# Seven products for the pooling gate, in a new product order, with stores on the POOL queue

## The chip, the cores and the metric

The kernel runs on one core of one Trainium2 chip. The metric is the device time of one execution in microseconds (us), lower is better. The core's engines have queues of their own and meet through semaphores: PE (TensorE, matmuls; PEld is its weight load), DVE (VectorE), ACT (ScalarE), POOL (GpSimd) and SP (SyncE, which here only issues transfers). ACT and POOL can issue transfers too.

## The reference

One decoder block on 1024 tokens of width 1024, in float32. Cut to what matters here:

```python
h = rms_norm(x, norm_gain) * (1.0 + scale) + shift
proj = h @ w_in
q, k, v, z_a, u, z_b, m_a, m_b = split(proj)          # 1024 columns each
p_a = (stick_breaking_attention(q, k, v) * silu(z_a)) @ w_branch_a
pooled = multiscale_causal_pool(u)    # window means over 2, 4, 8, 16 positions minus u, a linear map, a scale
p_b = (pooled * silu(z_b)) @ w_branch_b
merged = sigmoid(m_a) * p_a + sigmoid(m_b) * p_b
out = rms_norm(x + gate * (merged @ w_out), final_gain)   # gate comes from c, through w_gate
```

## The kernel before

Every large product is made of three float32r matmuls: both operands are split into a high part (a cast, on ACT) and a low part (the difference, on DVE), and high·high, high·low and low·high are added up in a PSUM bank. One matmul is 128 x 128 by 128 x 512.

After the norm the kernel goes through five stages, one behind the other on PE. They carry the names of their PSUM tiles in the profile:

- `u`: projection of the pooling input, copied out to DRAM (`u_d`) by ACT.
- `vp`: projection v, `mp`: projection m_b, each by `seven`: a 1024 x 1024 x 1024 product as Strassen and Winograd do it, with seven products of 512-blocks for eight. Its products are called p1 to p7.
- `wzb`: the pooling gate z_b, by `project`: all eight blocks, 16 x 24 = 384 matmuls. Beside it `make_d` forms the window differences d on DVE (log2 of the window adds on `win` tiles, L546, and a subtraction, L550), silu and the product with d follow per tile (L738, L739), and the sums of gate blocks that the next stage needs (`t1`, `t2`, L743 to L746). A product of w_gate's rows with silu(c) (`wg`, `sg`, L749 to L752) is spread over it.
- `bp`: pooled·silu(z_b) times w_branch_b, again `seven`; results go to DRAM as `pb_d`.

Behind them come the projections of q, k and the rest (`p`), the attention, and the output products.

In `seven(nm, sums, load, b_of, ...)` each product has two halves q = 0, 1 over the contraction, 24 matmuls each; the whole has 7 x 48 = 336. The operand a of a half is a quarter load (128 x 1024) or a sum of such loads, the operand b a quarter of h, of differences of h (`ht`), or of the gate. `raw(first, ...)` gives the tile for a load: with first = 1 from the tag `raw` in the pool `wts` (two buffers), otherwise from the tag `ar` in the stage's own pool (two buffers). The pool `vs` of v and m lies where the pool `first` lay, which holds the weights of u (`wg`). `a_op` makes the high and low part in a tile `whl` of two buffers (L559 the cast on ACT, L560 the difference on DVE), `b_op` the same for b (L565, L566). `copied` takes a PSUM bank to SBUF (ACT, L609), `added` adds one (DVE, L573), and `final` is the stage's own way out: `values` (vo, to `v_d`), `gate_b` (sigmoid, to `sb_d`), `branch` (to `pb_d`).

The order of the products is the loop's: p1, p5, p6, p7, p4, p3, p2. The order on each engine's queue is that of a scheduler which fills the queues from the program text by its own costs; only where the code says `keep_in_program_order` is it fixed. All loads and the stores v_d, sb_d, pb_d are issued on SP.

## Time and profile before

| | us |
|---|---|
| median of 3 runs (lowest, highest) | 1188.6 (1188.01, 1190.27) |
| the profiled execution | 1187.59 |
| its span in the profile | 1185.8 |
| PE busy | 1169.2 |
| DVE busy | 832.4 |
| ACT busy | 588.3 |
| POOL busy | 216.7 |
| mean granted TensorE clock | 0.998 of full speed |

The profile is that of one execution. Rows of a timeline give start, duration, engine, line, operation, out<-in with buffer numbers left out, and in brackets the idle time ahead of it with what ended it. Rows of groups give the busy time and the mean duration in ns of one instruction. Line L101 is that of a helper through which all matmuls and a few other operations go, so there the tile names tell them apart.

### The profile page before, as it was taken

To read this page: it belongs to the slowest core of one execution; us is meant where nothing else is said; L and a number is where in the kernel's file an instruction comes from. 1 tells how busy PE (TensorE), PEld (TensorE's weight loads), DVE (VectorE), ACT (ScalarE), POOL (GpSimd) and SP (SyncE) were. 2 spreads that over 40 slices of the span, in tenths; PEclk is the share of its full clock that TensorE was granted. 3 is DMA by queue.
4 is the path that set the end of the run, shared out by engine and by line. 5 is a ranking of instruction groups with operands and counts; after the bars stand their busy time and mean duration, and the time that the engine had idled before them with its cause. 6 is when DMAs were issued, how large, how long until landed. Compare 5 with 4: busy or idle time off the path is not lost.

```text
span 1185.8 us, 15373 instructions
## 1 busy us (share of the span) xinstructions
PE 1169.2 (99%) x5602; PEld 975.0 (82%) x5602; DVE 832.4 (70%) x1072; ACT 588.3 (50%) x1137; POOL 216.7 (18%) x248
## 2 busy tenths in 40 slices
PE   8999999999999999999999999999999999999997
...
GB/s 349 257 193 62 180 103 318 187 162 234 200 103 176 97 179 222 79 81 91 84 98 90 62 121 54 135 62 103 94 88 99 37 72 208 349 280 157 213 70 73
DMA packets 74750, 172.49 MB, mean 145 GB/s; under 512 B 9393, under 2 KB 22833, under 8 KB 72498
## 3 DMA queue, kind: packets, MB, share of 16 engines
q1 hardware_dynamic: 68770, 160.82, 41.6%
q10 hardware_dynamic: 5904, 10.68, 2.5%
...
## 4 chain that ended last, share of the span: by engine, by line
PE 84%; DVE 7%; DMA 3%; issue 3%; ACT 2%; SPq 0%; POOL 0%; POOLq 0%; DVEq 0%; ACTq 0%
PE p L101 24%; PE wzb L101 7%; PE mp L101 6%; PE vp L101 6%; PE bp L101 6%; PE o L101 6%; PE pa L101 5%; PE u L101 5%; PE z L101 5%; PE av L101 4%; PE wt L101 4%; PE ua L101 3%; DVE om L942 2%; DVE be L101 2%; PE wm L101 1%
## 5 line engine op out<-in xcount | busy, mean ns | idle before, releaser
L101 PE MATMUL p<-hT,w 128*128 128x512 f32 x1536 | 392.7, 392 | 1.3 <-DVE klo L101 1.3
L101 PEld LDWEIGHTS p<-hT,w 128*128 128x128 f32 x1536 | 283.0, 188 | 59.5 <-DVE klo L101 1.7
L942 DVE TENSOR_TENSOR_SCAN om<-om,eye 128x511 f32<-128x511 f32 (+7 forms) x128 | 184.0, 1442 | 68.9 <-ACT om L938 68.3
L149 POOL TENSOR_TENSOR w<-w_raw,w 128x256 fp32r<-128x256 f32 x124 | 124.8, 1037 | 571.5 <-ACT w L146 571.5
L938 ACT ACTIVATE om<-z 128x512 f32<-128x512 f32 (+2 forms) x192 | 95.0, 495 | 109.2 <-PE z L101 46.8
L962 DVE TENSOR_TENSOR wt<-wt,wt 128x512 fp32r<-128x512 f32 (+1 forms) x160 | 99.0, 619 | 15.7 <-ACT wt L961 14.7
L101 PE MATMUL av<-wt,vv 128*128 128x512 f32 x320 | 106.0, 412 | 0.1
L961 ACT CAST wt<-wt 128x512 fp32r<-128x512 f32 (+1 forms) x160 | 88.2, 551 | 35.0 <-PE wt L101 34.8
L101 DVE TENSOR_TENSOR be<-be,om 128x512 f32<-128x512 f32 (+7 forms) x128 | 98.5, 775 | 0.0
L101 PE MATMUL wt<-ident,be 128*128 128x128 f32 x576 | 90.3, 274 | 3.9 <-DVE wt L962 3.1
L939 ACT ACTIVATE be<-z 128x512 f32<-128x512 f32 (+2 forms) x192 | 94.0, 489 | 0.0
L101 PE MATMUL pa<-ga,wa 128*128 128x512 f32 x384 | 89.9, 390 | 0.9 <-DVE s L1115 0.8
L101 PE MATMUL o<-wo,mhl 128*128 128x512 f32 (+1 forms) x408 | 89.6, 377 | 0.0
L101 PE MATMUL wzb<-hT,wzb 128*128 128x512 f32 x384 | 87.2, 389 | 0.0
L101 PEld LDWEIGHTS pa<-ga,wa 128*128 128x128 f32 x384 | 71.9, 188 | 16.5 <-issue 1.2
L101 PEld LDWEIGHTS o<-wo,mhl 128*128 128x128 f32 x408 | 73.5, 188 | 14.1
L101 PEld LDWEIGHTS wt<-ident,be 128*128 128x128 f32 x576 | 69.5, 140 | 18.7 <-DVE wt L962 6.2
L101 PEld LDWEIGHTS wzb<-hT,wzb 128*128 128x128 f32 x384 | 72.1, 188 | 15.0
L991 POOL TENSOR_TENSOR tp<-tp,tl 128x256 f32<-128x256 f32 x32 | 38.1, 1190 | 153.9 <-DVE tp L988 153.9
L101 PE MATMUL z<-kl,q 128*128 128x512 f32 (+2 forms) x192 | 65.5, 341 | 0.0
L101 PE MATMUL z<-kh,q 128*128 128x512 f32 (+2 forms) x192 | 64.1, 334 | 0.0
L101 PE MATMUL u<-hT,wg 128*128 128x512 f32 x240 | 55.5, 391 | 0.0
...
## 6 DMA issues: line engine op xcount, KB each, us to landing
w_raw<-in_w_in SPq DMA_DIRECT2D x32, 512.0 KB, 3.5
v_d<-vo SPq DMA_DIRECT2D x16, 512.0 KB, 4.2
...
wa_raw<-in_w_branch_a SPq DMA_DIRECT2D x16, 512.0 KB, 4.7
...
va<-in_w_v SPq DMA_DIRECT2D x10, 512.0 KB, 4.0
ma<-in_w_mb SPq DMA_DIRECT2D x10, 512.0 KB, 4.4
```

What stands on the lines that cost most here:

```text
L101: ins = op(*args, **kw)
L149: gp.tensor_tensor(hl[:, 1, es], raw[:, es], hl[:, 0, es].bitcast(F32), op=ALU.subtract)
L938: act.activation(om[:, 1 + b0:1 + b0 + n], zp[:, :n], AF.Sigmoid, scale=-0.125)
L939: act.activation(be[:, b0:b0 + n], zp[:, :n], AF.Sigmoid, scale=0.125)
L942: v.tensor_tensor_scan(om[:, 1:W], om[:, 1:W], eye[:, :W - 1], 0.0, ALU.mult, ALU.max)
L961: act.copy(wt[:, 0, :off], pt[:, :off])
L962: v.tensor_sub(wt[:, 1, :off], pt[:, :off], wt[:, 0, :off].bitcast(F32))
L991: gp.tensor_add(tp, tp, tl)
```

## The change

- The gate z_b becomes a stage of `seven`, called z, with the tiles `zp…`; its results lie in four quarters (`g00` and three of the `ht` tiles), and b takes its operands from them (`g_parts`).
- The order of the products is p1, p2, p6, p7, p5, p4, p3. p1's a11 is loaded into an `ar` tile and kept: p6's operand is s2k = a22 − (a11 − a21), formed in `a_s2`, p7's is a11 − a21, p5's is s2k + a11, loaded once more as a11s. A stage has 14 quarter loads, before 18.
- Within a half the matmuls of the high parts of the first three (q = 0) or two (q = 1) output tiles come first.
- Stores of v, pb and g, and the loads of u, w_gate and d, are issued on POOL (`gp.dma_start`), stores of sb on ACT. A tick, a one-column POOL operation on a result of a given product (`beside`), comes ahead of each load of u and w_gate.
- The window differences are formed in stage v (3, 0, 2, 1) and stage m (5, 7, 6, 4), written to a new DRAM tile `d_d` and read back for z.

The diff, cut to its core:

```diff
@@ load_u, make_d
-        nc.sync.dma_start(u[:, :S], u_d[j])
+        tc.keep_in_program_order(gp.dma_start(u[:, :S], u_d[j]))
...
-        dhls[j] = d
+        gp.dma_start(d_d[j], d)
@@ seven
+        a11 = {}
+
+        def a_11(q):
+            a11[q] = raw(0, 0, 0, q, "a11")
+            return a11[q]
+
+        def a_s2(q):
+            r = raw(1, 1, 0, q, "a21")
+            v.tensor_sub(a11[q], a11[q], r)
+            r = raw(1, 1, 1, q, "a22s")
+            v.tensor_sub(k2(s2k, q), r, a11[q])
+            return k2(s2k, q)
+
         def a_s1(q):
-            r, w = raw(1, 1, 0, q, "a21"), raw(0, 1, 1, q, "a22")
-            v.tensor_add(r, r, w)
-            w = raw(0, 0, 0, q, "a11s")
-            v.tensor_sub(k2(s2k, q), r, w)
-            return r
-
-        def a_s3(q):
-            r, w = raw(1, 0, 0, q, "a11d"), raw(0, 1, 0, q, "a21d")
-            v.tensor_sub(r, r, w)
+            r = raw(1, 0, 0, q, "a11s")
+            v.tensor_add(r, r, k2(s2k, q))
             return r
...
-            p1=lambda q: raw(1, 0, 0, q, "a11"), p5=a_s1, p6=lambda q: k2(s2k, q), p7=a_s3,
-            p4=lambda q: raw(1, 1, 1, q, "a22"), p3=a_s4, p2=lambda q: raw(1, 0, 1, q, "a12"),
+            p1=a_11, p2=lambda q: raw(1, 0, 1, q, "a12"), p6=a_s2, p7=a11.get,
+            p5=a_s1, p4=lambda q: raw(1, 1, 1, q, "a22"), p3=a_s4,
...
-        for name in ("p1", "p5", "p6", "p7", "p4", "p3", "p2"):
-            c = {"p5": "b", "p3": "b", "p2": "c"}.get(name, "a")
+        for name in ("p1", "p2", "p6", "p7", "p5", "p4", "p3"):
+            c = {"p2": "c", "p5": "b", "p3": "b"}.get(name, "a")
...
+                ahead = 3 - q
+                parts_ = [(j, e, 0, 0) for j in range(ahead) for e in range(2)]
                 for j in range(4):
+                    for e in range(2):
+                        parts_ += [(j, e, w, m) for w, m in ((0, 0), (0, 1), (1, 0))[j < ahead:]]
...
+            for do in beside.get(name, ()):
+                gp.tensor_scalar(tick, mark[:, :1], 1.0, 0.0, op0=ALU.mult, op1=ALU.add)
+                do()
@@ stages
+        seven("v", vs, loads("w_v"), h_parts("v"), True, *banks, values, True, pooled(p1=(3,), p6=(0,), p7=(2,), p4=(1,)))
+        seven("m", vs, loads("w_mb"), h_parts("m"), False, *banks, gate_b, True, pooled(p1=(5,), p6=(7,), p7=(6,), p4=(4,)))
...
+        sg = gp_.tile([P, D], F32, name="sg")
+        nc.sync.dma_start(sg, a["c_row"].broadcast_to([P, D]))
+        act.activation(sg, sg, AF.Silu)
+
+        def modulated(j):
+            wg_ = gp_.tile([P, D], F32, tag="wg", bufs=2, name=f"wgt{j}")
+            tc.keep_in_program_order(gp.dma_start(wg_, a["w_gate"][j]))
+            v.scalar_tensor_tensor(wg_, wg_, 1.0, sg, ALU.mult, ALU.mult, accum_out=gate[:, j:j + 1])
...
+            def gate_z(m, n, j, src):
+                ct = 4 * m + j
+                ds = zg.tile([P, 512], F32, tag="ds", bufs=3, name=f"ds{ct}_{n}")
+                gp.dma_start(ds, d_d[ct][:, 512 * n:512 * n + 512])
+                z = gq[m, n][:, j]
+                act.activation(z, src, AF.Silu)
+                v.scalar_tensor_tensor(z, ds, psc_v[:, ct:ct + 1], z, ALU.mult, ALU.mult)
+                return z
+
+            seven("z", vs, loads("w_zb"), h_parts("z"), False, *banks, gate_z, True, rows(0, 1, 2, 3))
...
+        def g_parts(name, q):
+            g00, g01, g10, g11 = (k2(gq[k, n], q) for k, n in ((0, 0), (0, 1), (1, 0), (1, 1)))
+            x, y = k2(t1, q), k2(t2, q)
+            if name == "p6":
+                v.tensor_sub(x, g11, g01)
+                v.tensor_add(y, x, g00)
...
+        seven("b", vs, load_b_w, g_parts, False, *banks, branch, False, rows(4, 5, 6, 7))
```

In the rows below, a name is that of the stage, of the tile and its half, so `va11_0` is a11 of stage v for q = 0, and `waits` names the semaphores (DMAHW are those of hardware queues, DMASW those of software queues).

SP at the border from u to v, before:

```order
L693 DMA va11_0_1093<-in_w_v 128x1024 [waits DMAHW1_49,DVE_49]
L693 DMA va11_1_1122<-in_w_v 128x1024 [waits DMAHW2_49,DVE_49]
L693 DMA va21_0_1163<-in_w_v 128x1024 [waits DMAHW1_49,DMAHW0_49,DVE_49]
L693 DMA va21_1_1201<-in_w_v 128x1024 [waits DMAHW2_49,DVE_49]
L693 DMA va22_0_1165<-in_w_v 128x1024 [waits DMAHW5_49,PE_49]
L693 DMA va11s_0_1168<-in_w_v 128x1024 [waits DMAHW6_49]
```

And now:

```order
L718 DMA va12_0_1189<-in_w_v 128x1024 [waits DMAHW1_49,DVE_49]
L718 DMA va12_1_1218<-in_w_v 128x1024 [waits DMAHW2_49,DVE_49]
L718 DMA va11_0_1105<-in_w_v 128x1024 [waits DMAHW3_49,PE_49]
L718 DMA va11_1_1134<-in_w_v 128x1024 [waits DMAHW4_49]
L718 DMA va21_0_1267<-in_w_v 128x1024 [waits DMAHW5_49,DMAHW1_49,DVE_49]
```

The load that waits for PE (for the last matmul of u, whose weights lie in the space of the `ar` tiles) was that of a22, for p5; it is now that of a11, for p1, the stage's first product.

DVE in stage m, where the operands of the second and third product are made; before (p5 and p6):

```order
L587 TENSOR_TENSOR ma21_0_1722<-ma21_0_1722,ma22_0_1724 128x1024 [waits DMAHW3_49]
L573 TENSOR_TENSOR vs1_3_1157<-vp2_3_1568,vs1_3_1157 128x512 [waits PE_49]
L560 TENSOR_TENSOR mp1a1_1683<-ma11_1_1681,mp1a1_1683 128x1024 [waits DMAHW1_49,Activation_49]
L701 TENSOR_TENSOR vo2_0_1638<-vs1_2_1155,vo2_0_1638 128x8x64 [waits DMAHW2_49,Activation_49]
L589 TENSOR_TENSOR ms2k_1647<-ma21_0_1722,ma11s_0_1727 128x1024 [waits DVE_49]
L701 TENSOR_TENSOR vo3_0_1643<-vs1_3_1157,vo3_0_1643 128x8x64 [waits DMAHW4_49,Activation_49]
L560 TENSOR_TENSOR mp5a0_1730<-ma21_0_1722,mp5a0_1730 128x1024 [waits Activation_49]
```

And now (p2 and p6):

```order
L560 TENSOR_TENSOR mp2a1_1825<-ma12_1_1823,mp2a1_1825 128x1024 [waits DMAHW2_49,PE_49,Activation_49]
L546 TENSOR_TENSOR win5_1_1778<-u5_1775 128x1039 [waits DMASW0_49]
L546 TENSOR_TENSOR win5_2_1780<-win5_1_1778 128x1037 [waits DVE_49]
L597 TENSOR_TENSOR ms2k_1703<-ma22s_0_1871,ma11_0_1708 128x1024 [waits DMAHW4_49]
L546 TENSOR_TENSOR win5_4_1782<-win5_2_1780 128x1033 [waits DVE_49]
L595 TENSOR_TENSOR ma11_1_1737<-ma11_1_1737,ma21_1_1904 128x1024 [waits DMAHW5_49]
L573 TENSOR_TENSOR ms13_0_1766<-mp2_0_1790,ms13_0_1766 128x512 [waits PE_49]
L573 TENSOR_TENSOR ms13_1_1768<-mp2_1_1791,ms13_1_1768 128x512 [waits PE_49]
L560 TENSOR_TENSOR mp6a0_1874<-ms2k_1703,mp6a0_1874 128x1024 [waits Activation_49]
```

Window adds, which wait for a load on a software queue, stand between the steps of p6's operand, where results of the stage ahead stood between those of p5's.

ACT at the gate, before (wzb):

```order
L709 ACTIVATE sb3_0_2187<-ms1_3_1716 128x512 [waits DMAHW4_49,DVE_49,Activation_49]
L738 ACT_TABLE_LOAD
L738 ACTIVATE gb_2198<-wzb0_0_2220 128x512 [waits PE_49]
L749 ACTIVATE sg_2204<-sg_2204 128x1024 [waits DMAHW3_49]
L738 ACTIVATE gb_2198<-wzb0_1_2247 128x512 [waits PE_49]
L121 CAST wzb2_2367<-wzb2_raw_2365 128x1024
```

And now (stage z, between p2 and p6):

```order
L559 CAST zp2a1_2429<-za12_1_2427 128x1024 [waits DMAHW3_49,DVE_49]
L559 CAST zp6a0_2482<-zs2k_2319 128x1024 [waits DVE_49,PE_49,Activation_49]
L754 ACT_TABLE_LOAD [waits DMAHW4_49,DMASW5_49]
L754 ACTIVATE sg_2313<-sg_2313 128x1024 [waits DMASW1_49]
L772 ACTIVATE g00_1096<-zs13_0_2382 128x512 [waits DVE_49]
L772 ACTIVATE g00_1096<-zs13_1_2384 128x512 [waits DVE_49]
L772 ACTIVATE g00_1096<-zs13_2_2386 128x512 [waits DVE_49]
L772 ACTIVATE g00_1096<-zs13_3_2388 128x512 [waits DVE_49]
L559 CAST zp6a1_2518<-zs2k_2319 128x1024 [waits DVE_49,PE_49,Activation_49]
```

The table load and the silu of sg, which stood between two silus of the gate's first tile, now stand between the casts of p6's two halves, and the table load waits for sg's load.

More of the change, by code (lines that the diff above doesn't have):

```diff
@@ L81, in block_kernel @@
     u_d = dram.tile([KB, P, S], F32, name="u_d")
+    d_d = dram.tile([KB, P, S], F32, name="d_d")
     ident = idp.tile([P, P], F32, name="ident")
@@ L574, in added, with seven @@
         return t
-    def seven(nm, sums, load, b_of, a_moves, ta, tb, final, direct):
+    tick = spare[:, :1]
+    def seven(nm, sums, load, b_of, a_moves, ta, tb, final, direct, beside={}):
         s2k = sums.tile([P, 4, 512], F32, tag="s2k", bufs=1, name=nm + "s2k")
@@ L612, in seven @@
         chain, keep = {}, {}
[L613 to L614 removed]
+        for name in ("p1", "p2", "p6", "p7", "p5", "p4", "p3"):
+            c = {"p2": "c", "p5": "b", "p3": "b"}.get(name, "a")
             if c not in chain:
[L616 removed]
+                chain[c] = [bank((ta if c == "a" else tb)[j // 2], f"{nm}{name}_{j}") for j in range(4)]
             ps = chain[c]
@@ new lines, in seven @@
+                ends = {j: i for i, (j, *_) in enumerate(parts_)}
+                begun = set()
+                for i, (j, e, w, m) in enumerate(parts_):
+                    js = slice(j * P, j * P + P)
+                    l, r = (bl(m, e)[:, js], al[:, w, e]) if a_moves else (al[:, w, e, js], bl(m, e))
+                    mm(
+                        ps[j], l, r, start=name in ("p1", "p5", "p2") and q == 0 and j not in begun,
+                        stop=q == 1 and ends[j] == i, skip_group_check=True,
+                    )
+                    begun.add(j)
@@ L679, in block_kernel @@
         early.close()
+        tmps.close()
         vs = vps.enter_context(pool("vs", side="right"))
+        g00 = vps.enter_context(pool("gz", side="right")).tile([P, 4, 512], F32, name="g00")
+        diffs = ExitStack()
+        dif = diffs.enter_context(pool("dif", side="right"))
         def h_parts(nm):
@@ L729, in part @@
-    def part(src, k, n, q):
-        return src[:, 4 * k + 2 * q:4 * k + 2 * q + 2, 512 * n:512 * n + 512]
-    for j in range(KB):
-        if j not in dhls:
-            make_d(j, load_u(j))
-        def silu(sh, ps):
-            z = gb[:, j, sh * 512:sh * 512 + 512]
-            act.activation(z, ps, AF.Silu)
-            v.scalar_tensor_tensor(z, dhls[j][:, sh * 512:sh * 512 + 512], psc_v[:, j:j + 1], z, ALU.mult, ALU.mult)
-        project(CZB + j, f"wzb{j}", silu, act, v)
-        if j < 4:
-            v.tensor_sub(t1[:, j], gb[:, j, 512:], gb[:, j, :512])
-        else:
-            v.tensor_sub(t2[:, j - 4], gb[:, j, 512:], t1[:, j - 4])
-            v.tensor_sub(gb[:, j - 4, 512:], gb[:, j, 512:], gb[:, j - 4, 512:])
-        if j == 0:
-            nc.sync.dma_start(sg, a["c_row"].broadcast_to([P, D]))
-            act.activation(sg, sg, AF.Silu)
-        wg = pb.tile([P, D], F32, tag="wg", bufs=1, name=f"wg{j}")
-        nc.sync.dma_start(wg, a["w_gate"][j])
-        v.scalar_tensor_tensor(wg, wg, 1.0, sg, ALU.mult, ALU.mult, accum_out=gate[:, j:j + 1])
-        del dhls[j]
@@ L774, in branch, with pooled @@
-    def branch(m, n, j, t):
-        nc.sync.dma_start(pb_d[4 * m + j][:, 512 * n:512 * n + 512], t)
-    seven("b", sums, load_b_w, g_parts, False, ("av", "tr"), ("pj", "z"), branch, False)
-    pbs.close()
+            act.dma_start(sb_d[4 * m + j][:, 512 * n:512 * n + 512], t)
+            return t
+        banks = ("av", "tr"), ("pj", "z")
+        def pooled(**where):
+            return {name: [lambda j=j: make_d(j, load_u(j)) for j in js] for name, js in where.items()}
+        seven("v", vs, loads("w_v"), h_parts("v"), True, *banks, values, True, pooled(p1=(3,), p6=(0,), p7=(2,), p4=(1,)))
@@ new lines, in block_kernel @@
+        seven("m", vs, loads("w_mb"), h_parts("m"), False, *banks, gate_b, True, pooled(p1=(5,), p6=(7,), p7=(6,), p4=(4,)))
+        diffs.close()
+        gp_ = vps.enter_context(pool("gp_", side="right"))
+        gate = gp_.tile([P, KB], F32, name="gate")
+        bias = gp_.tile([P, KB], F32, name="gbias")
+        nc.sync.dma_start(bias, a["b_gate"])
+        sg = gp_.tile([P, D], F32, name="sg")
+        nc.sync.dma_start(sg, a["c_row"].broadcast_to([P, D]))
+        act.activation(sg, sg, AF.Silu)
@@ L781, in block_kernel, with branch @@
+        def branch(m, n, j, t):
+            gp.dma_start(pb_d[4 * m + j][:, 512 * n:512 * n + 512], t)
+            return t
+        seven("b", vs, load_b_w, g_parts, False, *banks, branch, False, rows(4, 5, 6, 7))
+        v.tensor_add(gate, gate, bias)
+        gp.dma_start(g_d[0].rearrange("(k p) -> p k", p=P), gate)
     logits = ExitStack()
```

91 lines of the change are left out of this document (37 added, 54 removed).

## Prediction

> **What bounds the kernel now.** I read the chain of work first, then the stretches of the five stages the diff touches, then the timelines of PE, SP, DVE and ACT around their borders. The chain says who sets the end (columns: start us, us, what):
>
> ```profile
> PE 84%; DVE 7%; DMA 3%; issue 3%; ACT 2%; SPq 0%; POOL 0%; POOLq 0%; DVEq 0%; ACTq 0%
> ...
> 80.79 48.07 PE u L101 x212
> 128.85 76.16 PE vp L101 x336
> 205.01 76.16 PE mp L101 x336
> 281.17 87.04 PE wzb L101 x384
> 368.21 75.56 PE bp L101 x330
> ...
> 447.35 8.51 DMA pb_d<-bs
> ```
>
> From 80.79 to 443.77 it is PE alone, one stage directly behind the other. The next view gives the four stages from v to b (length; then busy us of PE, PEld, DVE, ACT, POOL; granted clock; DMA share):
>
> ```profile
> 128.85:205.01 76.16, 76.16 (x338) 63.06 (x337) 51.70 (x55) 38.05 (x50) 0.00 (x0) 1.00 0.65 218
> 205.01:281.17 76.16, 76.16 (x338) 63.06 (x337) 43.09 (x44) 36.37 (x49) 0.00 (x0) 1.00 0.53 180
> 281.17:368.21 87.04, 87.04 (x386) 72.07 (x385) 72.98 (x106) 22.82 (x30) 0.00 (x0) 1.00 0.51 169
> 368.21:444.90 76.69, 76.69 (x337) 62.91 (x336) 49.20 (x48) 34.78 (x43) 2.84 (x4) 1.00 0.45 155
> ```
>
> PE is busy in every microsecond at clock 1.00, so a matmul removed here is time saved, and a wait added here is time lost, one for one. The gate's projection (wzb) is also where DVE is nearly full: 72.98 of 87.04. The only PE gap of the region is behind it, where the first key projection waits:
>
> ```profile
> 457.32 1.42 PE L101 MATMUL p<-hT,w 128*128 128x512 f32 x5 [1.26 <-DVE klo L101]
> ```
>
> **What goes.** The gate's 384 matmuls become 336. One costs 87.04/384 = 0.2267 us (76.16/336 is the same), so 48 fewer give −10.9 us. The 1.26 us gap goes too: the key cast that it hung on stands behind the store pb_d in the chain (8.51 us) and has no store to wait for now: −1.3.
>
> **Durations used below** (groups by line; mean ns is the second number after the bar):
>
> ```profile
> L559 ACT CAST mp6a<-ms2k 128x1024 fp32r<-128x1024 f32 x2 | 2.1, 1055 | 7.3 <-PE mp L101 7.3
> L738 ACT ACTIVATE gb<-wzb 128x512 f32<-128x512 f32 x16 | 9.6, 597 | 53.9 <-PE wzb L101 53.9
> L738 ACT ACT_TABLE_LOAD x1 | 1.3, 1283 | 0.0
> L749 ACT ACTIVATE sg<-sg 128x1024 f32<-128x1024 f32 x1 | 1.1, 1062 | 4.3 <-DMA sg<-in_c_row 4.3
> L739 DVE SCALAR_TENSOR_TENSOR gb<-d,vecs,gb 128x512 f32<-128x512 f32 x16 | 11.9, 746 | 7.5 <-ACT gb L738 7.5
> L546 DVE TENSOR_TENSOR win<-u 128x1039 f32<-128x1039 f32 x8 | 9.9, 1235 | 5.5 <-DMA u<-u_d 5.5
> L752 DVE SCALAR_TENSOR_TENSOR wg<-wg,sg 128x1024 f32<-128x1024 f32 x8 | 9.8, 1221 | 0.6 <-DMA wg<-in_w_gate 0.5
> L573 DVE TENSOR_TENSOR ms<-mp,ms 128x512 f32<-128x512 f32 x12 | 8.2, 690 | 2.4 <-PE mp L101 2.1 <-ACT ms L609 0.3
> L560 DVE TENSOR_TENSOR mp2a<-ma,mp2a 128x1024 fp32r<-128x1024 f32 x2 | 2.5, 1226 | 4.5 <-ACT mp2a L559 4.5
> 130.95 2.36 DVE L566 TENSOR_TENSOR vp5b<-ht,vp5b 128x1024 fp32r<-128x1024 f32 x2 [16.77 <-ACT vp5b L565]
> ```
>
> The last row, two full-width DVE operations in 2.36 us, says that they follow each other every 1.15 us. Loads (KB each, median us from issue to landing):
>
> ```profile
> va<-in_w_v SPq DMA_DIRECT2D x10, 512.0 KB, 4.0
> ma<-in_w_mb SPq DMA_DIRECT2D x10, 512.0 KB, 4.4
> u<-u_d SPq DMA_DIRECT2D x8, 512.0 KB, 4.7
> sg<-in_c_row SPq DMA_DIRECT2D x1, 512.0 KB, 6.7
> v_d<-vo SPq DMA_DIRECT2D x16, 512.0 KB, 4.2
> ```
>
> **Start of v: +5.4 us.** Before, p1's a11 lies in the weights' own `raw` buffers and is loaded well ahead; the load that must wait for the end of u is a22, which p5 needs 11 us later. Now p1's a11 is an `ar` tile in the space that the u weights hold, and its load waits for the last u matmul (128.86). Before's rows give what such a load takes when it is issued there: SP issue, first user on DVE, and the landing of this tile's loads in that window (min/median/max):
>
> ```profile
> 128.88 0.33 SPq L693 DMA_DIRECT2D va<-in_w_v  x1
> 133.23 1.22 DVE L587 TENSOR_TENSOR va<-va,va 128x1024 f32<-128x1024 f32 x1
> DMA to landing us min/median/max: 3.4/3.8/4.2
> ```
>
> 128.88 + 4.3 = 133.2, a cast of 1.05 and p1 starts at 134.3: PE idles 5.4 us (4.5 with the 3.4 us load). Nothing is left to cover it, since all of v stands behind p1.
>
> **The clock after that gap: +1.1 us.** The body of before has no gap this long, but its tail shows what idling does to the clock; PE's last matmuls there, and three half microseconds (granted clock third from the right):
>
> ```profile
> 1175.77 3.64 PE L101 MATMUL o<-wo,mhl 128*128 128x256 f32 x29
> 1181.00:1181.50 0.50, 0.00 (x0) 0.00 (x0) 0.12 (x1) 0.12 (x1) 0.34 (x1) 1.00 0.00 0
> 1181.50:1182.00 0.50, 0.00 (x0) 0.00 (x0) 0.43 (x1) 0.49 (x1) 0.00 (x0) 0.61 0.00 0
> 1182.00:1182.50 0.50, 0.00 (x0) 0.00 (x0) 0.00 (x0) 0.00 (x0) 0.00 (x0) 0.50 0.00 0
> ```
>
> The last matmul ends at 1179.41 and the clock is halved at about 1181.6, 2.2 us on. So v starts at half clock. How long that lasts no row shows. Bounds: nothing, or half speed for as long as the 5.4 us idle lasted (+2.7). I take as long as the fall took, 2.2 us at half speed, +1.1. The Trainium skill ("TensorE: Matmul & The Clock Gate", Part 1: The HAM clock gate) says that full clock returns after about 3.4 us of sustained work; by that the term would be +1.7 and the sum 0.6 higher.
>
> **p6 in each stage: +14.7 us.** Let T be the start of a stage's p1. A half product is 24 matmuls, 5.44 us; p1 ends at T+10.88, p2 at 21.76, p6's second half is due at 27.20. A half starts with its high parts (6 matmuls in the first half, 4 in the second), so its low part is due 1.6 to 2.3 us later. Before, p5 and its loads came second and p6's operand fell out of it. Now p6 comes third and its operand hangs on a chain through the two `raw` buffers that p2 holds: p2's first low part, load a21, subtract from a11, load a22 into the same buffer, subtract into s2k, cast. From the rows above: cast of p2a0 once p1's first half is done 5.5–6.55, low 7.8, load (4.0) 11.9, subtract 13.1, load 17.1, subtract 18.3, cast 19.4. That is 2.4 us ahead of 21.76. The second half: p2a1's low at 13.8, a21 at 17.8; a22 goes into the buffer that the first s2k frees, 18.3 to 22.3, subtract 23.5, cast 24.6: 2.6 us ahead of 27.20. So the chain alone fits. What stands between its rows on DVE and ACT does not:
>
> - z (gate). SP issues sg behind a22 at T+13.4; at 6.7 us it lands at 20.1. ACT, with sg's table load (1.3) and silu (1.06) in front of everything else, is free at 22.5. DVE stands at the product of w_gate's row 0 with sg until then. Behind it: that product 23.7, an add 24.4, a11−a21 25.6, two adds 26.9, one gate product 27.6, an add 28.25, s2k 29.4. Cast 30.45, where 27.20 was due: 3.25. Three gate products and an a11s add (3.4 us) pass before the low part, at 33.9, due at 32.7: 1.0 more. 4.2 us. ACT's table load alone costs half of it.
> - b. From the first add behind p3 of z (12 matmuls, 2.7 us, ahead of T) to p6a0's low part, DVE has 19 full-width operations, 8 adds and 4 gate products: 19 × 1.15 + 8 × 0.67 + 4 × 0.75 = 30.2 us, ending at T+27.5, due at 23.4. 4.1 us, with 0.1 or 0.2 for idle spots: 4.2.
> - m. Window adds of u5 stand ahead of s2k. u5 is fetched behind the tick at T+12 on POOL's queue; at 4.7 us it is there at 17. Two window adds 19.4, s2k 20.6, window add 21.8, a11 23.0, two adds 24.2, p6a0's low 25.4, due 23.4: 1.9. Then the difference, two adds and s2k: 29; and ACT casts mp7b first, which waits for p6's first half (29): 31.0 for the second cast, due 29.1: 1.9. 3.8 us.
> - v. As m with two window adds fewer ahead and the vo operations behind s2k: 1.2 and 1.3, 2.5 us.
>
> Bounds for this term: 0, if loads of 3.4 us and gaps on DVE give back what is missing; 18, with loads of 5.3. These gaps halve the clock too where one exceeds 2.2 us, but what follows is a wait for the low part, which covers slower high parts: 0. DVE gets back its lag in p7 and p5, whose casts come straight from s2k and the kept a11.
>
> **What else moves.** Loads and stores go to POOL. The page shows only hardware queues before:
>
> ```profile
> q1 hardware_dynamic: 68770, 160.82, 41.6%
> q10 hardware_dynamic: 5904, 10.68, 2.5%
> ```
>
> So a POOL transfer has no price here. Nearest rows: the same transfers from SP, 4.7 (u) and 4.2 (v_d); I take those, and as a far end that a load lands 5 us later. The Trainium skill ("DMA: Bandwidth & Descriptors", Anatomy of one DMA) fits such a transfer with 2.0 us and its bytes at 436 GB/s, as an estimate 3.2 us for u. By that, u5 is there at 15.2, the first wait of m falls to about 0.2, and the sum is 1.6 lower. The stores themselves are waited for by nobody near (vo has a buffer more). The 20 window adds (24.7 us at 1.235) that leave the gate stage for v and m cost nothing beyond the waits counted: p7, p5, p4 and p3 need one load at most, asked for a product ahead, so the cover there is p6 and p7 themselves (10.9 us each); without it m would pay its adds singly. Four loads fewer a stage shorten SP's queue, which PE does not wait for outside p1 and p6. The ticks run on POOL, which the stretches show idle (0.00). The 16 issues of sb_d move to ACT at 0.33 each (the SP row above), 5.3 us beside 36.37 of 76.16; the four that fall behind p2 stand in front of m's second p6 cast, which waits longer for s2k.
>
> **Sum.** −10.9 − 1.3 + 5.4 + 1.1 + 14.7 = +9.0 us. The profiled execution took 1187.6 with a span of 1185.8; it would be 1196.6. The median of the runs shown, 1188.6, is 1.0 above it, so I forecast 1197.6 for a median. The measurement tells 0.2% (2.4 us) from nothing.
>
> **Rivals.**
> 1. Faster: the p6 chain keeps pace, because loads come at 3.4 us and DVE finds its order without waiting. Each of the two loads in the chain then gives 0.6 us and the slack of 2.4 grows to 3.6; it decides where the rows in between delay s2k by less than that. For it speaks that before's p5 stood one product earlier with similar links and PE never waited; against it that DVE in b has no gap to catch up in. Then −5.7: about 1183.
> 2. No change: about half of the waits, 5 to 8 us, so that all in all it is between −2 and +2.4: 1187 to 1191. It takes DVE running ahead in z and b (4.2 each) but not in v and m.
> 3. Slower still: POOL's transfers land some 5 us late. u5 then holds DVE's queue in front of s2k to T+22 in m, similarly in v, and w_gate's row in z: up to 5 us in each of two or three stages, 1203 to 1210.
>
> **Chances.** Forecast with its own range 1191 to 1202: 0.50; rival 1: 0.20; rival 2: 0.17; rival 3: 0.13. Faster takes rival 1 and a little of 2 (0.22), no change most of 2 (0.16), slower the rest (0.62). The range from 1183 to 1205 leaves out the far end of rival 3 and the best end of rival 1.
>
> **What would show it.** After: a gate stage of 336 matmuls; a PE gap of about 5.4 us between u and vp with ACT's cast of vp1a as releaser, and a granted clock of 0.5 in the next 2 us; in each stage one or two PE gaps in front of p6a, released by ACT (cast) or DVE (low part), 2.5 to 4.2 us a stage, none in front of p7, p5, p4, p3; no gap at the first p. Wrong would be: no gap at v's p1 (a load issued earlier than the order says), p6 gaps under 1 us, or a long DVE wait on the u loads from POOL.

## The result and the profile after

The changed kernel takes 1227.14 us (median of 4 runs, 1225.7 to 1228.4) against 1189.24 of the kernel before on the same chip: a ratio of 1.0319, interval 1.0301 to 1.0337. It is 38 us slower, where the forecast was 9 slower. The profiled execution took 1225.7 with a span of 1223.8, and the differences below are those of the spans (1223.8 − 1185.8 = 38.0). Two of the ten executions of c11, further down, were slow (1544.75 and 3015.65 us): its median is over all ten, its ratio leaves them out.

The four stages v, m, z, b after, in the view that the prediction shows of before (PE, PEld, DVE, ACT, POOL busy; clock; DMA share; GB/s):

```profile
128.66:217.90 89.24, 79.44 (x337) 63.99 (x337) 62.77 (x74) 40.16 (x51) 15.08 (x23) 0.98 0.57 192
217.90:305.11 87.21, 80.56 (x337) 64.81 (x336) 63.84 (x73) 38.43 (x51) 9.29 (x16) 0.96 0.61 210
305.11:389.26 84.15, 78.07 (x337) 64.19 (x336) 59.51 (x67) 40.90 (x52) 12.56 (x25) 0.96 0.54 184
389.26:474.49 85.23, 78.70 (x337) 63.79 (x336) 62.80 (x68) 36.47 (x45) 20.98 (x26) 0.96 0.40 139
```

Each stage has 336 matmuls, worth 76.16 us at full clock; each takes 8 to 13 us longer. DVE is busy for 59 to 64 us of a stage, so neither DVE nor another engine beside PE is full: the time is in waits. The chain of work names what they end on:

```profile
PE 71%; DVE 11%; DMA 8%; issue 4%; ACT 3%; POOL 1%; SPq 0%; POOLq 0%; ACTq 0%; DVEq 0%
...
128.66 3.98 DMA va<-in_w_v
...
171.85 6.86 DMA u<-u_d
...
184.86 6.00 DMA u<-u_d
...
230.24 5.13 DMA u<-u_d
...
289.82 6.72 DMA sb_d<-sb
...
320.05 8.26 DMA sg<-in_c_row
...
401.15 5.69 POOL spare L659
...
406.84 5.77 DMA wgt<-in_w_gate
...
482.64 13.67 DMA kl<-klo
```

From u to the end of b before was PE alone; now loads of u and of w_gate, stores of sb and POOL's tick (`spare`) stand between its pieces, and so do loads of operands that are left out above (`va`, `va22s`, `za`). PE's rows with the longer gaps in brackets; the second row, without a gap, shows what 24 matmuls take at full clock:

```profile
133.76 12.79 PE L102 MATMUL vp<-vp1a,hT 128*128 128x512 f32 x48 [5.13 <-ACT vp1a L559]
157.27 5.60 PE L102 MATMUL vp<-vp6a,vp6b 128*128 128x512 f32 x24
196.93 5.53 PE L102 MATMUL vp<-vp4a,vp4b 128*128 128x512 f32 x23 [2.24 <-DVE vp4b L566]
249.43 7.34 PE L102 MATMUL mp<-mp6b,mp6a 128*128 128x512 f32 x24 [2.49 <-ACT mp6a L559]
298.21 7.07 PE L102 MATMUL mp<-hT,mp3a 128*128 128x512 f32 x24 [2.94 <-ACT mp3a L559]
338.55 6.68 PE L102 MATMUL zp<-zp6b,zp6a 128*128 128x512 f32 x21 [6.08 <-ACT zp6a L559]
417.27 4.30 PE L102 MATMUL bp<-bp6b,bp6a 128*128 128x512 f32 x11 [6.00 <-ACT bp6a L559]
497.18 11.62 PE L102 MATMUL p<-hT,w 128*128 128x512 f32 x39 [6.21 <-DVE klo L102]
```

A gap costs more than its bracket, since the next matmuls run at a lower clock: the 24 of 249.43 take 7.34 us for 5.60. The granted clock (third from the right) over these matmuls in m and those behind z's gap:

```profile
249.43:256.61 7.18, 7.18 (x25) 5.75 (x26) 3.68 (x5) 2.67 (x4) 0.00 (x0) 0.76 0.61 228
338.55:345.75 7.20, 7.20 (x25) 5.81 (x26) 6.46 (x7) 3.61 (x5) 1.36 (x3) 0.76 0.76 242
```

So I take a product's cost from the starts of neighbouring products, less 10.88 us for 48 matmuls. A wait ahead of p6 counts with p6. The 38 us come out so:

| part | us |
|---|---|
| 48 matmuls fewer | −10.9 |
| gap ahead of v's p1, and the clock behind it | 5.1 + 1.7 |
| p6's operands: v 2.2, m 6.1, z 8.0, b 9.1 | +25.4 |
| v's p5 and p4 | +4.0 |
| m's p4 and p3 | +5.0 |
| gap ahead of a key projection, 6.2 now and 1.3 before | +5.0 |
| first p to first z beyond that gap | +2.4 |
| first z to first pa (attention) | +2.1 |
| pa to the end, and the end of u | −1.2 |
| 0.6 that b lost before | −0.6 |

That adds up to 38.0. The 2.4 is clock: the 39 matmuls of 497.18 take 11.62 us, and the 1536 projection matmuls take 2.5 us more in all, in the groups of before and after:

```profile
L101 PE MATMUL p<-hT,w 128*128 128x512 f32 x1536 | 392.7, 392 | 1.3 <-DVE klo L101 1.3
L102 PE MATMUL p<-hT,w 128*128 128x512 f32 x1536 | 395.2, 394 | 6.2 <-DVE klo L102 6.2
```

The attention's 2.1 shows as waits of the `wt` matmuls (5.7 us in all against 3.9). Its cause is open. From the first z to the first pa all runs below take 533.5 to 536.1 us, with the gap at the projections or without it, where before took 531.7; so it comes from something that all of them keep. One such thing is not in the cut diff: the loads of vv are fixed in program order now.

One profile is one execution, and single waits vary. Up to the gate's store, the run e_gd below has the same order on DVE, ACT, POOL and SP as the changed kernel, yet in it v's p5 and p4 lose 5.5 in place of 4.0, m's p4 and p3 2.1 in place of 5.0, and the clock behind v's gap costs 2.6 in place of 1.75. A difference of up to 3 us in one place is therefore no proof of what an edit did.

What stands behind the gaps is read on the other engines. Rows of DVE, ACT and POOL:

```profile
190.89 1.24 DVE L546 TENSOR_TENSOR win<-u 128x1039 f32<-128x1039 f32 x1 [4.89 <-DMA u<-u_d]
246.23 1.26 ACT L735 ACTIVATE sb<-ms 128x512 f32<-128x512 f32 x2 [3.05 <-DMA sb_d<-sb]
296.63 0.60 ACT L735 ACTIVATE sb<-mp 128x512 f32<-128x512 f32 x1 [5.78 <-DMA sb_d<-sb]
330.78 1.23 DVE L759 SCALAR_TENSOR_TENSOR wgt<-wgt,sg 128x1024 f32<-128x1024 f32 x1 [4.34 <-ACT sg L754]
401.15 5.74 POOL L659 TENSOR_SCALAR spare<-bs 128x1 f32<-128x1 f32 x1 [11.43 <-ACT bs L617]
406.84 0.58 POOL L758 DMA_DIRECT2D wgt<-in_w_gate  x1
405.62 1.22 DVE L566 TENSOR_TENSOR bp2b<-ht,bp2b 128x1024 fp32r<-128x1024 f32 x1
412.63 1.23 DVE L759 SCALAR_TENSOR_TENSOR wgt<-wgt,sg 128x1024 f32<-128x1024 f32 x1 [5.79 <-DMA wgt<-in_w_gate]
496.43 0.69 DVE L102 TENSOR_TENSOR klo<-p,kh 128x512 fp32r<-128x512 f32 x1 [14.99 <-DMA kl<-klo]
```

- v: DVE stands 4.89 us for a load of u with p4's operands queued behind that window add.
- m: the sigmoid on ACT waits for a buffer that the store of sb still holds, 3.05 us ahead of p6's second cast and 5.78 us ahead of p3's cast. There are two such buffers now, three before (`go` in `gate_b`, not in the cut diff). Of the 3.05 at most 0.5 counts: between them and p6's cast stands that of mp7b, whose buffer is free only when p6's first half ends on PE, at 246.94, and it began at 247.40.
- z: sg's load is issued at 320.05 and takes 8.26 us. DVE waits until 330.78 at the first product with sg, and the second s2k follows only at 336.12.
- b: the tick of one column, 0.18 us where DVE leaves room, takes 5.74 us. Until it ends at 406.89 DVE works without a pause, to 406.84 (its last row); only then is the load of w_gate issued, and DVE stands 5.79 us for it ahead of p6's operands.
- Projections: DVE stands 14.99 us for a buffer (`kl`) whose store took 13.67 us. Ahead of it, at 473.76, the gate vector g went out as 1024 single words of 4 bytes; the same store stood at 343.2 before, inside wzb.

### The profile page after: what moved, and what is told of

It reads as the page before. It is cut to its first block, busy times and chain, and to the rows that moved or that the text cites. A ratio compares the mean times of both kernels' runs of the same rounds, so it can differ in the third digit from the quotient of the medians.

```text
span 1223.8 us, 15413 instructions
## 1 busy us (share of the span) xinstructions
PE 1172.4 (96%) x5554; PEld 972.4 (79%) x5554; DVE 862.1 (70%) x1100; ACT 610.8 (50%) x1163; POOL 276.4 (23%) x337
## 4 chain that ended last, share of the span: by engine, by line
PE 71%; DVE 11%; DMA 8%; issue 4%; ACT 3%; POOL 1%; SPq 0%; POOLq 0%; ACTq 0%; DVEq 0%
PE p L102 22%; PE pa L102 7%; PE o L102 6%; PE bp L102 4%; PE u L102 4%; PE z L102 4%; PE av L102 4%; PE zp L102 4%; PE wt L102 4%; PE mp L102 4%; PE ua L102 3%; DVE om L969 2%; PE vp L102 2%; DMA u<-u_d 2%; DMA kl<-klo 2%
## 5 line engine op out<-in xcount | busy, mean ns | idle before, releaser
L102 PEld LDWEIGHTS u<-hT,wg 128*128 128x128 f32 x240 | 44.8, 188 | 9.6 <-issue 0.5
L102 PEld LDWEIGHTS av<-wt,vv 128*128 128x128 f32 x320 | 48.5, 191 | 0.7 <-DVE wt L989 0.7
```

The source lines that it names most:

```text
L102: ins = op(*args, **kw)
```

## Experiments

Theory: the waits come from DVE's queue in order, in which operations that depend on a load issued late (u, w_gate, sg) stand ahead of p6's operand; the g store's place makes the projection's gap. Rivals: p6's loads (two buffers of `raw`) set the time by themselves, the POOL queue's transfers are slow, or the new product order costs whatever stands in it.

All ratios are against before, measured along with each run (1187.3 to 1189.3 us):

| run | what differs from the changed kernel | us | ratio (interval) |
|---|---|---|---|
| after | | 1227.14 | 1.0319 (1.0301–1.0337) |
| e_a11 | p1's a11 in tiles of its own | 1216.86 | 1.0247 (1.0230–1.0264) |
| e_notick | no ticks | 1208.72 | 1.0179 (1.0164–1.0194) |
| e_nowin | no window differences | 1204.23 | 1.0134 (1.0119–1.0149) |
| e_nomod | no products of w_gate and sg | 1210.42 | 1.0188 (1.0173–1.0203) |
| c_old | product order of before in v and m | 1204.54 | 1.0125 (1.0109–1.0140) |
| e_stores | stores back on SP | 1225.13 | 1.0299 (1.0263–1.0335) |
| c2 | e_a11 and no ticks | 1201.54 | 1.0095 (1.0073–1.0116) |
| c_old_nts | c_old, no ticks, stores on SP | 1198.36 | 1.0077 (1.0062–1.0092) |
| e_r2 | p6's a21 in two buffers of its own | 1207.81 | 1.0167 (1.0140–1.0193) |
| c3 | c_old_nts with g's store on POOL | 1199.53 | 1.0092 (1.0077–1.0107) |
| c4 | c3 and buffers for a21 in z and b | 1190.41 | 1.0024 (1.0014–1.0034) |
| e_gd | g stored as 8 rows | 1218.56 | 1.0251 (1.0231–1.0271) |
| c6 | c4, g as rows, w_gate later, ticks in z and b | 1188.83 | 1.0010 (0.9996–1.0024) |
| c7 | c6 with ticks in m too | 1184.10 | 0.9965 (0.9950–0.9979) |
| c9 | new order; e_a11, e_r2 and e_gd together | 1195.25 | 1.0055 (1.0036–1.0074) |
| c11 | c9 without ticks | 1188.87 | 1.0001 (0.9981–1.0020) |
| c8 | c7 with w_gate's last two rows earlier | 1180.82 | 0.9930 (0.9916–0.9944) |

**e_a11: the start of v.**

```diff
-            t = (wts if first else sums).tile(... tag="raw" if first else "ar" ...)
+            t = (wts if first else ars[0]).tile(...)      # a pool opened ahead of u
```

> The changed kernel with one edit: the two tiles that hold p1's a11 get a place of their own that the u weights never used, so the first loads of v can leave before u ends. Theory (the gap at the border and the half clock behind it are one cost, nothing else hides behind them): 5.1 us of PE gap and 1.75 us of slow p1 go, 1227.1 - 6.9 = about 1220. Rival (another operand is late by as much, p2's or p6's chain simply starts to bind): under 3 us, 1224 or more.

The gap is gone, and the clock loss with it:

```profile
128.65 11.04 PE L102 MATMUL vp<-vp1a,hT 128*128 128x512 f32 x48
```

10.3 us in place of 6.9: besides the start's 6.8, m's p4 and p3 lost 1.6 in place of 5.0, and v's p5 and p4 6.6 in place of 4.0, differences of the size that e_gd shows without an edit there. The place of the tile is shown as the cause of the first gap.

**e_notick: the ticks.**

```diff
-                gp.tensor_scalar(tick, mark[:, :1], 1.0, 0.0, op0=ALU.mult, op1=ALU.add)
```

> The changed kernel without the ticks: the one-column POOL operations ahead of the loads of u and of w_gate's rows are left out, so that these loads leave as soon as a buffer is free. Theory (DVE stands in order behind window adds and gate products whose loads leave too late, and one tick took 5.7 us itself): b's p6 gap loses 5 to 6, v's p5 and p4 3.8, m's p6 1 to 2, the start of the key projections 2 to 3: about 1214. Rival (p6's own chain of two loads through the two buffers is what is late): the p6 gaps stay, 1222 or more. Rival (POOL's transfers are slow in themselves): no change.

18.4 us. b's p6 went from 9.1 to 2.8, z's from 8.0 to 3.3, v's from 2.2 to 0.1, v's p5 and p4 from 4.0 to 2.2. But m's p6 stayed at 6.0, and a wait opened at its p7 (2.1): loads issued earlier bring their window adds ahead of operands that are due sooner. The projection's gap stayed (6.3).

**e_nowin: the window differences.** ds is loaded from u_d, so the window means are left out.

```diff
-        seven("v", ..., values, True, pooled(p1=(3,), p6=(0,), p7=(2,), p4=(1,)))
-        seven("m", ..., gate_b, True, pooled(p1=(5,), p6=(7,), p7=(6,), p4=(4,)))
+        seven("v", ..., values, True)
+        seven("m", ..., gate_b, True)
```

> The changed kernel without the window differences: no u loads, window adds and stores of d in v and m; the gate multiplies u itself, so this part of the computation is left out. Theory (window adds that wait for u hold DVE's queue): v's p5 and p4 lose their 3.8 us of gaps, p6 of v 1 and of m 4 to 5, z's p6 1: 1227 - 10 = about 1217. Rival (p6's chain by itself): p6 keeps its gaps in v and m, only the 3.8 go, 1223.

23 us: v lost 0.2 behind its start (after: 6.2), m 1.0 (after: 11.1). z lost nothing either, though its own operations are the same apart from where ds is read. So what the window adds cost is not only their waits in v and m: they shift the loads behind them.

**e_nomod: the products with sg.** The gate is the bias alone here.

```diff
-        act.activation(sg, sg, AF.Silu)
-            seven("z", ..., rows(0, 1, 2, 3))
+            seven("z", ...)
-        seven("b", ..., rows(4, 5, 6, 7))
+        seven("b", ...)
```

> The changed kernel without the modulation gate: no sg load and silu and no products with w_gate's rows in z and b (the gate is left at its bias). Theory (these rows hold ACT and DVE in front of p6's operands): z's p6 loses 6 of 8.0 us, b's 6 of 9.1, the start of the key projections 3: about 1212. Rival (p6's chain by itself, and DVE too full in b): z's and b's gaps stay above 5 each, 1222.

16.7 us: the wait ahead of b's p6 is gone (2.2 is left inside it), and so is the projection's gap, since the store of g, which no longer waits for the products, moved to 323.38, into z. There it did what it had done at the projections: a load of a11s issued at 327.94 came 9 us later, and z's p6 lost 10.4.

```profile
337.33 1.23 DVE L602 TENSOR_TENSOR za11s<-za11s,zs2k 128x1024 f32<-128x1024 f32 x1 [4.03 <-DMA za11s<-in_w_zb]
```

**c_old: the order of before in v and m alone.**

```diff
-        seven("v", ...)
-        seven("m", ..., *banks, ...)
+        seven_old("v", ...)       # p1, p5, p6, p7, p4, p3, p2; 18 loads; the order before within a half; vo in 3 buffers
+        seven_old("m", ..., *sknab, ...)
```

> The changed kernel with the old order of the seven products (p1, p5, p6, p7, p4, p3, p2) and its 18 quarter loads in v and m alone; z and b keep the new order (a store buffer less and two tiles more for it). Theory (the new order is what puts two loads, one behind the other, between p2 and p6): v's gap at the start and its half clock go (6.9), p6's gaps of v and m go (2.2 and 6.1), the window adds' waits stay: 1227 - 13 = about 1214. Rival (the window adds block DVE whatever the order): only the start, 1220.

22.6 us. v lost 3.9 in place of 13 and m 3.6 in place of 11; z also fell, to 4.3, as it fell with e_nowin. The order of the products, the loads and the order of the matmuls within a half go back together here, so none of the three is shown by itself.

**e_stores: the stores.**

```diff
-            gp.dma_start( v_d ...        -            gp.dma_start(pb_d ...
+            nc.sync.dma_start( v_d ...   +            nc.sync.dma_start(pb_d ...
-            act.dma_start(sb_d ...       -        gp.dma_start(g_d ...
+            nc.sync.dma_start(sb_d ...   +        nc.sync.dma_start(g_d ...
```

> The changed kernel with the stores of v, sb, pb and g back on SP (loads of u, w_gate and d, and the store of d, stay on POOL). Theory (at the start of the key projections POOL makes weights' low parts and issues stores in one queue, and in m ACT stands in front of stores it issues itself): the 6.2 us gap there falls to 1 to 2, m's p3 loses 3 to 5 of its 5.0: about 1218. Rival (SP's loads now stand behind stores that wait for DVE): p6's gaps grow by as much, 1227 or more.

About 2 us, within the two intervals. The projection's gap fell to 3.1 and m's p4 and p3 to 1.4, but m's p1 and p2 now lost 2.1 and 3.5 and b's p3 4.4. On SP's queue loads of operands now stand behind stores: six of v's are issued from 211.56 on, and m's next load of an operand leaves only at 229.24. That is the rival's mechanism.

**c2 and c_old_nts: what the first findings give together.**

```diff
 c2 = e_a11 + e_notick
 c_old_nts = c_old + e_notick + e_stores
```

> Both single edits together: p1's a11 in a place of its own, and no ticks. Theory (separate causes): 1227.1 - 10.3 - 18.4 = 1198. Rival (they hide one another, since both make DVE late in v): 1205 or more.

> The old order in v and m, no ticks, and the stores of v, sb, pb and g on SP. Theory (order 13, ticks 12 beyond v and m's p6, stores 5 to 8): about 1195, with gaps left in b's p6 (2 to 3) and in front of z's p6 (2 to 3). Rival (the windows' work itself is too much beside v and m): 1205 or more.

Both miss by 3 us. In c2 p6 and p7 of m still lose 5.8 and 3.7, and the projection's gap grows to 9.2. In c_old_nts that gap is gone but b's p6 loses 16.0 (12.1 behind its start). The store of g is again at its place: issued on SP at 389.14, with the load of a11s behind it at 391.69:

```profile
404.99 1.23 DVE L602 TENSOR_TENSOR ba11s<-ba11s,bs2k 128x1024 f32<-128x1024 f32 x1 [8.18 <-DMA ba11s<-in_w_branch_b]
```

**c3: does the queue of that store matter?**

```diff
-        nc.sync.dma_start(g_d ...
+        gp.dma_start(g_d ...
```

> The old order in v and m, no ticks, the stores of v, sb and pb on SP, but the store of g (single words) back on POOL. Theory (that store held up the loads behind it on SP: 13 us for a11s in b): b's p6 loses 9 to 10 of its 12.1, 1198 - 9.5 = about 1189. Rival (the products with w_gate's rows are what is late in b): 1196 or more.

No: b's p6 loses 14.6 (10.7 behind its start) with the store on POOL too. In five microseconds while it is under way the DMA engines are all busy (share 1.05) and move 61 GB/s:

```profile
395.00:400.00 5.00, 4.82 (x21) 3.97 (x22) 2.40 (x3) 2.49 (x3) 0.00 (x0) 1.00 1.05 61
404.05 1.23 DVE L602 TENSOR_TENSOR ba11s<-ba11s,bs2k 128x1024 f32<-128x1024 f32 x1 [6.65 <-DMA ba11s<-in_w_branch_b]
```

**e_r2: the buffers of p6's chain.**

```diff
-            r = raw(1, 1, 0, q, "a21")
+            r = sums.tile([P, 2, 512], F32, tag="r2", bufs=2, ...); load(r, 1, 0, q)
```

> The changed kernel with two tiles of their own for p6's first load (a21), so that it leaves while p1 runs and need not wait for p2's low part (for the room one store buffer of v and one of d less). Theory (p6's operands are late because two loads stand one behind the other in the buffers that p2 holds, and the DVE order leaves no room for it): the gaps at p6 halve, v 1, m 3, z 4, b 5: about 1227 - 12 = 1215. Rival (what makes p6 late is only work that waits in DVE's queue, window adds and w_gate's rows): within 4 of 1227.

For the room the edit also takes a buffer from vo and one from d. 19 us. p6's waits fell from 25.4 to 14.4 (v 0, m 3.7, z 3.0, b 7.7) and v's p5 and p4 from 4.0 to 0.6, so the rival that the two `raw` buffers set the time has a part of it: a load that need not wait for p2's low part comes sooner, and the operations queued behind it too.

**c4: the same buffers with the old order in v and m.**

```diff
 c3, and in z and b
-            r = raw(1, 1, 0, q, "a21")
+            r = extra[0].tile([P, 2, 512], F32, tag="r2", bufs=2, ...); load(r, 1, 0, q)
```

> As the one before, and a21 of p6 in z and b in tiles of its own (one buffer for w_gate's rows instead of two). Theory: z's and b's p6 come without a gap, 4 us less than the one before, about 1185; with that it is faster than the kernel before (1188.6). Rival (single buffer for w_gate's rows makes DVE wait): 1190 or more.

1190.4 where 1185 was expected: b's p6 fell from 14.6 to 4.2, but z's p7 opened with 4.5, behind a product of w_gate that waits for its load. The rows of w_gate have one buffer here in place of two, and the rival had named that.

**e_gd: the form of g's store.**

```diff
-        gp.dma_start(g_d[0].rearrange("(k p) -> p k", p=P), gate)
+        transpose(gt[:KB, :P], gate); act.copy(gs, gt[:KB, :P])
+        gp.dma_start(g_d[0].rearrange("(k p) -> k p", p=P), gs)      # 8 rows of 512 B
```

> The changed kernel with one edit: the gate vector is transposed on PE first, so that its store to DRAM writes eight rows of 512 bytes instead of 1024 single words. Theory (that store keeps the DMA engines busy for some ten microseconds, and the moves of the first keys' low parts lie behind it): the 6.2 us PE gap at the start of the key projections falls under 2, 1227 - 5 = about 1222. Rival (the 1 MB load of v issued just ahead on SP is what they lie behind): no change, 1226 or more.

8.6 us. At the projections 6.21 became 0.29, though 2.96 opened at the first z; from the first p to the first z it takes 29.0 us in place of 34.1. In the profiled execution some 2 us more were gained ahead of the store, where the edit changes nothing.

```profile
494.69 3.70 PE L102 MATMUL p<-hT,w 128*128 128x512 f32 x15 [0.29 <-DVE qlo L102]
...
501.36 0.47 PE L102 MATMUL z<-kh,q 128*128 128x512 f32 x1 [2.96 <-DMA q<-qlo]
```

Between 470 and 500 the lists of transfers (KB each, median us to landing) and the stretches of after show how the words act (`after` stands for the changed kernel):

```profile
pb_d<-bs POOLq DMA_DIRECT2D x4, 256.0 KB, 13.1
kh<-kh SPq DMA_DIRECT2D x6, 128.0 KB, 10.8
g_d<-gate POOLq DMA_DIRECT2D x1, 4.0 KB, 12.3
```

```profile
480.00:485.00 5.00, 5.00 (x24) 4.14 (x23) 0.69 (x1) 0.59 (x1) 4.37 (x7) 1.00 0.86 31
485.00:490.00 5.00, 5.00 (x24) 4.14 (x23) 0.00 (x0) 1.62 (x3) 2.82 (x4) 1.00 0.90 264
490.00:495.00 5.00, 0.97 (x5) 0.47 (x3) 0.00 (x0) 0.59 (x1) 0.00 (x0) 1.00 1.02 307
```

The same list with rows (e_gd):

```profile
pb_d<-bs POOLq DMA_DIRECT2D x4, 256.0 KB, 2.5
g_d<-gs POOLq DMA_DIRECT2D x1, 4.0 KB, 4.4
```

The words are under way for 12.3 us, and in the five from 480 on little moves (31 GB/s at a DMA share of 0.86); then what has queued up behind them, b's last stores, key stores and a load of vv, runs off at 264 to 307 GB/s, and kl's store lands at the end of that. As rows the store takes 4.4 us. It is still issued ahead of kl's stores (at 477.76, they from 480.25 on). The rival has a part: kl's stores behind vv's load of 1 MB land after 6.65 and 7.03 us here, and after 6.21 in e_nomod, where the words are far off and the gap is gone too; ahead of it one lands after 4.75. With words and vv ahead it was 13.67. For b's last stores (2.5 in place of 13.1) the comparison is not clean: they leave ahead of the rows, where they left behind the words. By what means the words hold up the rest is open: before, with next to nothing else to move, their store took 11.7 us too, at a DMA share of 0.14 and 0.15 (345 to 355). The Trainium skill ("DMA: Bandwidth & Descriptors", Specifications) names 512 B as the least transfer for the line rate, which fits: the rows are 512 B each, the words 4.

**c6, c7 and c8: a version with these findings.**

```diff
 c6: c4 + e_gd; w_gate's rows at p6, p7, p5, p4; ticks in z and b only
 c7: as c6, ticks in m too
 c8: as c7
-        seven("b", ..., rows(4, 5, 6, 7))                       # p6, p7, p5, p4
+        seven("b", ..., rows(p6=(4,), p7=(5, 6), p5=(7,)))
```

> Old order in v and m, stores on SP, a21 in tiles of its own in z and b, the gate vector stored in rows, no ticks in v and m; in z and b the products with w_gate's rows keep their ticks, but begin behind p6 instead of p1. Theory (those rows stand ahead of p6's and p7's operands on DVE): z's 4.5 and b's 4.1 go, 1190.4 - 8 = about 1182, faster than before (1187.3). Rival (DVE is too full around b's p6 without them): 1187 or more.

> As the one before, with the ticks back in m. Theory (without them window adds are pulled ahead of m's p5 operands, 4.5 us there): 3 us less than the one before, about 1179. Rival (with them the loads of u come too late again, as in the changed kernel): 2 to 4 more than the one before.

> The mended kernel with the old order in v and m, ticks in m, z and b, and w_gate's last row moved from p4 to p5 (rows 5 and 6 both behind p7): the row whose load DVE waited 5.55 us for ahead of p3's operands in b is now asked for one product earlier. Theory (the gap ahead of b's p3 of 4.4 us is that load): -4 us to about 1180. Rival (the two rows behind p7 share DVE's time with p5's operands, so the wait moves to p5 or p4): same, 1183 to 1185.

c6 is level with before, 7 us above what was expected: z's and b's p6 do lose only 0.5, but b's p3 opened with 4.1. c7 is 0.35% faster than before. Without a tick in m its p5 lost 4.3, with ticks nothing, though p6 then lost 2.1: a tick that holds a load back helps where the window add would else stand ahead of p5's operand. c7 was left with 4.4 us at b's p3 (a gap of 2.45 and the clock behind it), where DVE waits 5.55 us for w_gate's last load but one:

```profile
427.20 1.23 DVE L834 SCALAR_TENSOR_TENSOR wgt<-wgt,sg 128x1024 f32<-128x1024 f32 x1 [5.55 <-DMA wgt<-in_w_gate]
```

With this load and the last one a product earlier each (c8) DVE waits 0.52 us for this one and 2.07 us for the last, and b's p3 loses 0.3; the first row is DVE's, the others are the stages v, m, z and b:

```profile
425.59 1.23 DVE L834 SCALAR_TENSOR_TENSOR wgt<-wgt,sg 128x1024 f32<-128x1024 f32 x1 [2.07 <-DMA wgt<-in_w_gate]
127.67:203.91 76.24, 76.24 (x338) 63.02 (x336) 58.99 (x70) 37.58 (x49) 3.21 (x6) 1.00 0.72 236
203.91:282.99 79.08, 77.45 (x338) 62.71 (x336) 62.08 (x69) 37.30 (x49) 5.39 (x11) 1.00 0.67 231
282.99:360.60 77.61, 76.60 (x337) 62.87 (x336) 58.96 (x69) 41.35 (x54) 15.75 (x24) 1.00 0.65 217
360.60:437.64 77.04, 76.80 (x338) 62.95 (x337) 62.42 (x68) 36.86 (x47) 8.74 (x14) 1.00 0.43 142
```

The four stages take 310.0 us (before 316.1 from v to b's end, after 345.8), 5.3 above four times 76.16. c8 is 0.70% faster than before (0.56 to 0.84), the best of all.

**c9 and c11: is it the order or the places?** Both keep the new order in all four stages.

```diff
 c9 = e_a11 + e_r2 + e_gd
 c11 = c9 + e_notick
```

> The changed kernel with its own product order kept and three places mended: a11 of p1 in tiles of its own, p6's a21 in two buffers of its own, g written as rows of 512 B. Theory (each of the three gaps has a cause of its own, and what the ticks and window adds cost comes on top): 1227 - 10.3 - 19 - 8.6 = 1189 if the three gains add up. Rival (DVE's in-order queue with loads issued behind ticks is the shared cause, so that a mended gap opens further on, as p7's and p6's in m did without ticks): 1196 to 1203, with gaps in m's p6 and p3 and in z's and b's p6 or p5.

> As the kernel ahead of it here, and without the ticks. Theory (a tick delays a load until a product's result is there, and POOL's tick itself waits beside DVE's two-input operations, so its removal helps where DVE waits for the load): 4 to 8 us below it, 1185 to 1195. Rival (without ticks the loads are issued as early as buffers are free, and window adds and w_gate products stand ahead of p6's operand in m and z, as p7's wait in m without ticks showed): same or up to 4 us above it.

c9 gains 32 us where its three edits singly gain 38.2: it misses both expectations and lies just below the rival's. It still loses 7.4 at b's p6, and the cause is the tick again, now 7.51 us long, while DVE worked to 388.65 and then stood for w_gate:

```profile
381.18 7.51 POOL L661 TENSOR_SCALAR spare<-bs 128x1 f32<-128x1 f32 x1 [9.05 <-ACT bs L619]
387.43 1.22 DVE L796 TENSOR_TENSOR ht<-ht,g 128x1024 f32<-128x1024 f32 x1
392.35 1.23 DVE L762 SCALAR_TENSOR_TENSOR wgt<-wgt,sg 128x1024 f32<-128x1024 f32 x1 [3.70 <-DMA wgt<-in_w_gate]
```

Without ticks b's p6 loses 0.9 (c11), and 6.4 us go, as the theory had it. What is left in c11 is m: p6 2.2 and p5 4.6, of which the latter is a window add whose load comes 5.76 us late ahead of p5's operands:

```profile
249.79 1.24 DVE L546 TENSOR_TENSOR win<-u 128x1039 f32<-128x1039 f32 x1 [5.76 <-DMA u<-u_d]
```

So all 38 us go while the order stays: the order alone isn't the loss. The gate's −10.9 is still paid back in waits there: v 0.9, m 7.5, z 3.1, b 1.0. Whether the 8 us between c11 and c8 are the old order in v and m isn't settled, since the two differ in ticks, stores and w_gate's places too.

Added up, seven single edits (e_a11, e_notick, e_nowin, e_nomod, c_old, e_r2, e_gd) gain 119 us, and all there was to gain was 38 and the gate's 10.9. They overlap: one gap has several conditions, and taking away any of them closes it.

## Why the prediction was right or wrong

Right: the direction; 48 matmuls at 0.2267 us (each stage has 336, and they take 10.88 a product); the gap at v's p1 by the load of a11, 5.13 for 5.4, shown by e_a11; and p6 in each stage as a place of waits. Luck: v's p6, 2.2 for 2.5. The forecast had 1.2 in the first half and 1.3 in the second; measured are none in the first and gaps of 0.57 and 1.02 in the second.

The clock behind the gap was 1.75 for 1.1 (12.63 us from p1 to p2 for 10.88); over the seven runs with that gap it was 1.7 to 2.9. The Trainium skill's 3.4 us of sustained work ("TensorE: Matmul & The Clock Gate", Part 1: The HAM clock gate) gave 1.7, the better figure for this trace and the low end of the seven.

Wrong, by 29 us in all:

- **p6 in each stage, 14.7 → 25.4.** The size was wrong in three stages, and one step is wrong in all three: "These gaps halve the clock too … 0". The granted clock was 0.76 over 7.18 us behind m's gap, 0.76 over 7.20 behind z's and 0.88 over the 13.70 us of b's p6; by that slower matmuls cost 1.7, 1.7 and 1.6, some 5 us in all (in m 24 matmuls took 7.34 us for 5.60 behind a gap of 2.49). m: its gaps, 0.43, 0.67 and 2.49, come to 3.6 where the step had 3.8, so what m lost beyond the term (2.3) is mostly clock. z: sg landed 8.26 us after its issue, not 6.7, and was issued 1.5 later; of the 3.8 that z lost beyond the term, these are 3.1; the clock took the place of the 1.0 forecast for the low part, for which PE did not wait. (ACT's table load is not half of the 4.2, as the step says: it is 1.28 us, and only with the silu is it 2.3.) b: the term counted operations on DVE to T+27.5; in fact DVE stood 5.79 us for w_gate behind a tick of 5.74 us.
- **"DVE gets back its lag in p7 and p5" and "cost nothing beyond the waits counted": 0 → 9.0.** In v's p5 and p4 it doesn't: loads of u issued behind a tick at 171.85 and 184.86 come 6 to 7 us later, and DVE's queue keeps p5's and p4's operands behind them. In m's p4 and p3 it is "The stores themselves are waited for by nobody near" that failed: ACT stands 5.78 us for a buffer of sb ahead of p3's cast. Without the window adds both waits are 0 (e_nowin); how the adds make m's store late isn't shown.
- **"No gap at the first p": −1.3 → +5.0, and 2.4 of clock.** The prediction followed the key cast's store buffers, and not where the g store goes: from the middle of a full stage to just ahead of the projections. e_gd shows the store's form as the cause of the late key stores.
- **"The ticks run on POOL, which the stretches show idle": 0.** In b a tick lasted as long as the dense run of DVE's operations beside it; the cost lies inside b's p6 above. e_notick gained 18.4, and c11 over c9 6.4.
- Attention, 2.1: not foreseen, cause open. The other parts come to −1.5 (pa to the end, the end of u, b's own 0.6, the start of v).

Rival 3 named a load held in front of DVE's queue, with the POOL queue's transfers as the cause and 5 us of delay. The mechanism was right and the cause wrong: such a load landed after 5.1 us in the median (u, 512 KB) where SP's took 4.7 (the prediction's other estimate, 3.2 us, was not reached). It was the issue that came late. A sign that the prediction named for being wrong, a long DVE wait on the u loads from POOL, did show: 4.89 us in v.
